# Probabilities times values of a forgetting attention: one plain fp32 pass in two halves of the array in place of a split in high and low parts

## The chip, the cores and the metric

One NeuronCore of a Trainium2 chip (trn2) runs the whole program. The metric is the device time of one execution in microseconds (us); lower is better. Engines are named as the profile names them: PE (TensorE, matmuls), PEld (its weight loads), DVE (VectorE), ACT (ScalarE), POOL (GpSimd), SP (the queue that issues most DMAs).

## What is computed

The reference is one layer of a hybrid block over 2048 tokens of width 1024, all in float32: RMSNorm, one wide input projection, and three branches (a forgetting attention, a complex state-space layer with a gated unit, a cross-attention into 256 memory tokens), which are gated, projected, merged and added to the input. The change lies in the forgetting attention, with 12 heads of width 64:

```python
def block(args):                                   # 128 queries of all heads
    qi, Fi, s0 = args
    s = jnp.einsum('bhqd,bhkd->bhqk', qi, kh)
    s = s + Fi[..., None] - F[:, :, None, :]       # F: running sum of log forget gates
    s = jnp.where(key_pos[None, :] <= qpos[:, None], s, NEG)
    p = jax.nn.softmax(s, axis=-1)
    return jnp.einsum('bhqk,bhkd->bhqd', p, vh)    # the product that is changed
```

## The kernel before

**Precision.** Nearly every product is done with operands split into two float32r parts, high and low (`hi` is a copy in that type, `lo` the rest). `mm3` (L147 to L149) issues hi*hi, hi*lo and lo*hi into one sum in PSUM. These three lines are most of the program's matmuls.

**Stages.** The input projection fills the first part; the state-space branch, its gated unit and the memory attention ride along in it. Then the forgetting attention runs, with the last projection chunks (`gen_gl`) and a first part of the merge (`gen_merge0`) as filler between its steps, and the rest of the merge and the output projection end the program. The forgetting attention holds 1628 to 2540 us of the span in the profile below.

**The attention.** `gen_fox` goes through heads and, in a head, through groups G = 7 to 0 of 256 queries, so 96 groups. For a group, `fox_scores` makes two blocks of 128 queries: matmuls into `psA` (L750, L751), the bias and the row maximum on DVE (L752), the exponential on ACT (L757), the division on POOL (L761). One group later `fox_pv` multiplies the probabilities with the values. It takes the keys in pairs `kp` of two tiles of 128 keys (even tile a = 0, odd tile a = 1), G + 1 pairs for group G, so 432 pairs in the program:

- PE transposes the probabilities of a pair into `psB` (L782; up to four transposes of 128x128).
- ACT copies them as high parts into `Pt` (L785; L790 for the last pair, which the causal mask cuts), and DVE subtracts to get the low parts (L786, L791).
- PE multiplies per key tile (L798): the weights are the tile's values `v`, 64 columns of high parts beside 64 of low parts; what streams is 512 columns of `Pt`, high parts of 256 queries, then low parts. All four products of parts land in the 128 partitions of `psC`; 864 matmuls, one for each key tile. For the last odd tile only the later 128 queries are streamed (256 columns).
- At the end of a group the four quarters are added: L801 (ACT), L802 (DVE), L804 (ACT), L805 (POOL); then comes the gate (L806, POOL) and a DMA.

In this stage `psA` and `psB` have three buffers, `psC` has one (`PS2`). The values are written to DRAM by `proj_v` (48 DMAs `s_vs<-ev_v`) and read back by `fox_keys` (24 DMAs `v<-s_vs`).

**What sets the order.** Each engine runs its own instructions in program order. The code's generators interleave attention and filler by constants (`PACE`, `LAG`, `DUE`), and the tile framework then orders each engine's instructions by a simulated timeline, so a change of one operation moves others too.

**A place that the prediction uses.** In `s5_pair` of the state-space branch a plain fp32 product already runs with 64 columns of weights, its results in the lower and the upper half of PSUM's partitions (L583 to L586):

```python
for g in range(2):
    for ri in range(2):
        nc.tensor.matmul(pv[64 * g:64 * g + 64, ri * 256:(ri + 1) * 256],
                         m1t[:, ri * 128 + 64 * g:ri * 128 + 64 * g + 64], u[:, g, :], start=True, stop=True)
```

All four are 128x64 weights by 128x256 data; the calls run 24 times, so these are 96 matmuls, and the trace has 192 instructions of them: a plain fp32 matmul is carried out as two. In the program's order the four of a call stand together four times; in the other 20 calls the two small matmuls of L572 (16 columns of weights) stand between, 14 times after the second of them, 6 times after the first. L625 and L626 are plain fp32 products over the full 128 columns.

Of the kernel before, what the change touches and what calls it, by code (L numbers as in the profile page):

```python
# [49 lines left out]
class Layer:  # L50
# [17 lines left out]
    def setup(self):  # L68
        nc, i = self.nc, self.i
        self.const, self.close_const = self.pool("const", side="right")  # L70
        self.wp, self.close_wp = self.pool("wp", side="right")
        self.ps, self.close_ps = self.pool("ps", space=PSUM)
        c = self.const
        self.eps = c.tile([128, 1], F32, name="eps")
        nc.vector.memset(self.eps, EPS)
        warm = c.tile([128, 1], F32, name="warm")
        nc.scalar.activation(warm, self.eps, AF.Sqrt)
        self.ident = c.tile([128, 128], F32, name="ident")
        nc.scalar.dma_start(out=self.ident, in_=i["ident"])
        self.g1 = c.tile([128, KD], F32, name="g1")  # L80
        nc.scalar.dma_start(out=self.g1, in_=i["g_norm"])
        self.identb = c.tile([128, 128], BF16, name="identb")
        nc.vector.tensor_copy(self.identb, self.ident)
        pw = self.psC()
        for n in range(WARM):
            nc.tensor.matmul(pw[:, :128], self.identb, self.identb, start=True, stop=True)
        s = {}
        for n, sh, dt in (
            ("qh", [DF, L], F32), ("ql", [DF, L], F32), ("kh", [DF, L], F32), ("kl", [DF, L], F32),
            ("vs", [H, 16, 128, 128], F32), ("gf", [DF, L], F32), ("gs", [DF, L], F32),  # L90
            ("gl", [3 * D, L], F32), ("gm", [DM, L], F32), ("qmh", [DM, L], F32), ("qml", [DM, L], F32),
            ("u", [6, 8, 128, 256], F32), ("kd", [48, 16, 128], F32), ("nf", [H, L], F32), ("yx", [DF, L], F32), ("yc", [6, 8, 128, 256], F32),
            ("ys", [DF, L], F32), ("ym", [DM, L], F32),
            ("mkh", [128, HM, ML], F32), ("mkl", [128, HM, ML], F32),
            ("mvh", [128, 2, DM], F32), ("mvl", [128, 2, DM], F32),
        ):
            s[n] = self.dram("s_" + n, sh, dt)
        self.s = s
# [35 lines left out]
    def load_w(self, src, shape, pool=None, bufs=2):  # L134
        """One [128, 1024] slab of weights, split into two float32r parts."""
        raw = self.wp.tile([128, 4 * NV], F32, tag="wraw", name="wraw", bufs=2)
        k, m = shape
        n = k * m
        self.nc.sync.dma_start(out=raw[:, :n], in_=src)
        hi, lo = ((pool or self.wp).tile([128, n if bufs == 1 else 1024], F32R, tag=t, name=t, bufs=bufs) for t in ("whi", "wlo"))  # L140
        self.split(hi[:, :n], lo[:, :n], raw[:, :n])
        return (hi[:, :n].rearrange("p (k m) -> p k m", k=k), lo[:, :n].rearrange("p (k m) -> p k m", k=k))

    def mm3(self, out, a, b, first, last):
        """a = (hi, lo) stationary, b = (hi, lo) moving."""
        nc = self.nc
        nc.tensor.matmul(out, a[0], b[0], start=first, stop=False)  # L147
        nc.tensor.matmul(out, a[0], b[1], start=False, stop=False)  # L148
        nc.tensor.matmul(out, a[1], b[0], start=False, stop=last)  # L149

    def rsqrt(self, p, out, ssq, n):
        """out = 1 / sqrt(ssq / D + eps): table square root, then a Newton step."""
# [11 lines left out]
    def norm_T(self, src, nt, g, hi, lo, p, xb, split=False):  # L164
        """RMSNorm of nt tiles of 128 tokens, then transposed and split: hi, lo [128, KD, nt*128]."""
# [90 lines left out]
    def proj_v(self, g, p):  # L256
        """Values of four heads; the forget gates ride with the first four."""
# [5 lines left out]
        for t in range(16):  # L263
# [7 lines left out]
            o = self.ev.tile([128, 4, 128], F32R, tag="ehi", name="ev_v", bufs=2)  # L271
            pv = ps[:, :256].rearrange("p (h d) -> p h d", h=4)
            nc.scalar.copy(o[:, :, 0:64], pv)
            nc.vector.tensor_sub(o[:, :, 64:128], pv, fl32(o[:, :, 0:64]))
            nc.sync.dma_start(out=s["vs"][g * 4:(g + 1) * 4, t].rearrange("h p d -> p h d"), in_=fl32(o))
# [12 lines left out]
    def forget(self, p):  # L288
        """-F, the running sum of -log sigmoid(z)."""
# [118 lines left out]
    def s5_exp(self, p, out, x):  # L408
        """exp(x): range reduction by ln 2, polynomial, exact power of two."""
# [15 lines left out]
    def s5_reduce(self, t, n):  # L425
        """t - 2 pi round(t / 2 pi), in place."""
        v = self.nc.vector
        v.tensor_scalar(out=n, in0=t, scalar1=0.15915494309189535, scalar2=12582912.0, op0=ALU.mult, op1=ALU.add)
        v.tensor_scalar(out=n, in0=n, scalar1=-12582912.0, scalar2=None, op0=ALU.add)
        for c in (6.28125, 2029.0 / 1048576.0, 3.0199159819e-7):  # L430
            v.scalar_tensor_tensor(out=t, in0=n, scalar=-c, in1=t, op0=ALU.mult, op1=ALU.add)

    def s5_sincos(self, p, sn, cs, t, n):
        """sin and cos of t in [-pi, pi] (t is overwritten) by the quarter angle and two doublings."""
# [17 lines left out]
    def cmul(self, outr, outi, ar, ai, br, bi, t):  # L452
        """(outr, outi) = (ar, ai) (br, bi); t is scratch; the outputs are none of the inputs."""
# [8 lines left out]
    def s5_prep(self, q, p):  # L462
        """Discretised parameters in the layout [(group parity, state), group pair]; q keeps, p is scratch."""
# [70 lines left out]
    def s5_pair(self, q, a):  # L534
        """Groups 2a and 2a+1. Chunks of 8 steps: what a chunk adds to the state (M1), the state at each chunk's
        end (a real scan of the states turned back by the phase they have run through), and the outputs from the
        state before the chunk (M2) and from the chunk's own inputs (M3)."""
# [168 lines left out]
    def fox_keys(self, h, c):  # L706
        """Half a head's keys (high over low parts), values (high beside low) and -F."""
# [3 lines left out]
        v = p.tile([128, 8, 128], F32R, tag="v", name="v", bufs=3)  # L711
# [4 lines left out]
        nc.sync.dma_start(out=fl32(v), in_=s["vs"][h, c * 8:(c + 1) * 8].rearrange("t p d -> p t d"))  # L716
# [13 lines left out]
    def fox_scores(self, p, hd, q, G, P):  # L730
        """Softmax rows of two blocks of 128 queries, the later one first: the mask goes into -F for good, as no
        later block of queries is left to read those keys unmasked."""
# [32 lines left out]
    def fox_pv(self, p, h, hd, G, P):  # L765
        """Columns of the moving operand and of the sums: high parts of the two query blocks, then low parts."""
# [6 lines left out]
        for kp in range(G + 1):  # L773
            ps = self.psB()
            t = p.tile([128, 2, 512], F32R, tag="Pt", name="Pt", bufs=3)
            hi, lo = t[:, :, 0:256], t[:, :, 256:512]
# [6 lines left out]
            psv = ps.rearrange("p (a n) -> p a n", a=2)  # L783
            if kp < G:
                nc.scalar.copy(hi, psv)  # L785
                nc.vector.tensor_sub(lo, psv, fl32(hi))  # L786
            else:
                for a in range(2):
                    c = slice(a * 128, 256)
                    nc.scalar.copy(hi[:, a, c], psv[:, a, c])  # L790
                    nc.vector.tensor_sub(lo[:, a, c], psv[:, a, c], fl32(hi[:, a, c]))  # L791
            for a in range(2):
                kt = 2 * kp + a
                v = hd[kt // 8][1][:, kt % 8, :]
                o, m = po, t[:, a, :]
                if kt == 2 * G + 1:
                    o, m = (z.rearrange("p (x b n) -> p x b n", x=2, b=2)[:, :, 1, :] for z in (o, m))
                self.pe = nc.tensor.matmul(o, v, m, start=(kt == 0), stop=(kt == 2 * G + 1))  # L798
            yield
        t = p.tile([128, 256], F32, tag="ot", name="ot", bufs=1)  # L800
        nc.scalar.copy(t, po[:, 256:512])  # L801
        nc.vector.tensor_add(t, po[:, 0:256], t)  # L802
        o = p.tile([64, 256], F32, tag="oo", name="oo", bufs=2)
        nc.scalar.copy(o, t[64:128])  # L804
        nc.gpsimd.tensor_add(o, o, t[0:64])  # L805
# [3 lines left out]
    def gen_fox(self):  # L809
        """Heads one after the other, groups of queries from the last to the first; a head's last KS groups, the  # L810
        short ones, alternate with the next head's first ones."""
# [75 lines left out]
    def split(self, hi, lo, x, sc=1.0):  # L887
        """sc * x as hi + lo, each exact in float32r."""
# [8 lines left out]
    def ytile(self):  # L897
        """Slots of 4 KB, twelve in the first pool and ten in the second, in the order in which they come free."""
# [21 lines left out]
    def gen_merge0(self):  # L920
        """The last chunk, under the last heads; its share of the attention as soon as the last head is past it."""
# [131 lines left out]
# The channels of the state-space branch are kept, 128 at a time, in the order (channel of a group, group).  # L1053
# [69 lines left out]
```

## Time and profile before

| what | us |
|---|---|
| median of 3 runs | 3076.02 (3070.25 to 3080.53) |
| the profiled execution: span from first to last instruction | 3072.7 |
| PE busy | 2995.7 (97% of the span) |
| DVE, ACT, POOL busy | 1884.8, 927.8, 1004.8 |
| L798, the matmuls that are replaced | 864 instructions |

For the profiled execution the page gives the span alone; the median of the timed runs is 3.3 us above it. A row of a group reads: line, engine, operation, output <- inputs, partitions x elements, count, busy us, mean ns of one; then the idle time of the engine ahead of it. A row of the timeline reads: start, duration, engine, line, operation, operands, weights' rows * columns, data's partitions x columns, count of merged neighbours. Matmuls are pipelined: the duration of one (some 0.39 us for 512 columns) overlaps the next, so what a matmul costs on PE is the distance from its start to the next one's start.

### The profile page before, as it was taken

Reading aid. Unit: us, or ns where it says so; the run is one execution under the profiler, and the core shown is the slowest. Engines: PE = TensorE matmul, PEld = TensorE weight load, DVE = VectorE, ACT = ScalarE, POOL = GpSimd, SP = SyncE. Lnnn points to the kernel's source line nnn. Section 1 sums busy time; section 2 is a strip of 40 time slices with the busy share of each in tenths; the row PEclk is TensorE's granted clock in tenths of the full one; section 3 lists DMA queues with packets and bytes.
Section 4 is the critical chain, followed back from the end, with each engine's and each line's share of the span. In section 5 each row is a group of like instructions: output and inputs, shape, how many; then the busy total and the mean of one; then the engine's idle time right before and its main releaser. Section 6 shows DMA issues by size and latency. Waiting matters only on the chain.

```text
span 3072.7 us, 43527 instructions
## 1 busy us (share of the span) xinstructions
PE 2995.7 (97%) x14656; PEld 2438.1 (79%) x14656; DVE 1884.8 (61%) x4982; ACT 927.8 (30%) x1881; POOL 1004.8 (33%) x1328
## 2 busy tenths in 40 slices
PE   9999999999999999999999999999999998999999
PEld 7889977777777778888878888888887786777787
DVE  5333489888886673322217777777777886555544
ACT  5102111111112231222216666666666550000011
POOL 0010000000001332121205665655555766555500
PEclk9999999999999999999999999999999998999999
DMA  5343323323344655344352443544434536665531
GB/s 167 107 136 96 105 84 116 115 84 111 114 132 150 175 164 173 108 127 136 115 165 82 124 121 103 134 121 121 118 111 130 145 108 195 185 182 172 159 108 69
DMA packets 283118, 396.81 MB, mean 129 GB/s; under 512 B 83060, under 2 KB 147828, under 8 KB 282884
## 3 DMA queue, kind: packets, MB, share of 16 engines
q1 hardware_dynamic: 275696, 381.39, 41.8%
q10 hardware_dynamic: 7200, 12.66, 1.2%
q8 instruction: 116, 1.90, 0.3%
q14 instruction: 106, 0.87, 0.1%
HBM read 265.51 MB, written 128.42 MB: 128 GB/s over the span
## 4 chain that ended last, share of the span: by engine, by line
PE 80%; DMA 6%; DVE 5%; issue 4%; POOL 3%; ACT 1%; SPq 0%; DVEq 0%; POOLq 0%; ACTq 0%
PE psF L147 10%; PE psF L148 10%; PE psF L149 10%; PE psA L147 8%; PE psA L148 8%; PE psA L149 8%; PE psC L798 5%; PE psB L782 5%; PE psA L750 3%; PE psA L751 3%; PE psC L147 1%; PE psC L148 1%; PE psC L149 1%; PE psC L585 1%; PE psB L149 1%
## 5 line engine op out<-in xcount | busy, mean ns | idle before, releaser
L147 PE MATMUL psF<-hh,whi 128*128 128x512 f32 (+1 forms) x1160 | 470.2, 405 | 5.3 <-DVE elo L228 2.5
L889 POOL TENSOR_SCALAR whi<-wraw 128x1024 fp32r<-128x1024 f32 (+2 forms) x216 | 204.8, 949 | 795.2 <-PE psA L148 362.0
L149 PE MATMUL psF<-hh,wlo 128*128 128x512 f32 (+1 forms) x1160 | 460.5, 397 | 0.5 <-DVE wlo L891 0.5
L148 PE MATMUL psF<-hl,whi 128*128 128x512 f32 (+1 forms) x1160 | 460.7, 397 | 0.0
L891 DVE TENSOR_TENSOR wlo<-wraw,whi 128x1024 fp32r<-128x1024 f32 (+2 forms) x216 | 260.5, 1207 | 213.4 <-POOL whi L889 189.2
L147 PE MATMUL psA<-hh,whi 128*128 128x512 f32 (+1 forms) x816 | 322.5, 397 | 1.4 <-ACT hh L187 0.8
L148 PE MATMUL psA<-hl,whi 128*128 128x512 f32 (+1 forms) x816 | 322.9, 396 | 0.0
L149 PE MATMUL psA<-hh,wlo 128*128 128x512 f32 (+1 forms) x816 | 321.7, 395 | 0.8 <-DVE wlo L891 0.8
L786 DVE TENSOR_TENSOR Pt<-psB,Pt 128x512 fp32r<-128x512 f32 x336 | 226.2, 685 | 76.3 <-ACT Pt L785 73.9
L798 PE MATMUL psC<-Pt,v 128*128 128x512 f32 x864 | 266.7, 398 | 4.1 <-DVE Pt L786 3.5
L147 PEld LDWEIGHTS psF<-hh,whi 128*128 128x128 f32 x1160 | 219.6, 189 | 52.7 <-DVE elo L228 3.3
L149 PEld LDWEIGHTS psF<-hh,wlo 128*128 128x128 f32 x1160 | 219.5, 189 | 52.0 <-DVE wlo L891 0.9
L148 PEld LDWEIGHTS psF<-hl,whi 128*128 128x128 f32 x1160 | 219.8, 189 | 45.8 <-issue 0.4
L752 DVE CUSTOM_DVE_ANT_0 P<-psA,nf 128x512 f32<-128x512 f32 (+1 forms) x336 | 201.2, 627 | 48.1 <-PE psA L751 28.2
L785 ACT CAST Pt<-psB 128x512 fp32r<-128x512 f32 x336 | 191.9, 586 | 107.4 <-PE psB L782 60.4
L761 POOL TENSOR_SCALAR P<-P,rd 128x768 f32<-128x768 f32 (+1 forms) x240 | 193.2, 821 | 59.6 <-DVE rd L758 36.6
L750 PE MATMUL psA<-kk,qh 128*128 128x512 f32 (+1 forms) x480 | 184.1, 389 | 4.5 <-DVE mx L752 2.6
L147 PEld LDWEIGHTS psA<-hh,whi 128*128 128x128 f32 x816 | 154.1, 189 | 36.9 <-issue 1.6
L149 PEld LDWEIGHTS psA<-hh,wlo 128*128 128x128 f32 x816 | 154.5, 189 | 36.1 <-DVE wlo L891 1.2
L148 PEld LDWEIGHTS psA<-hl,whi 128*128 128x128 f32 x816 | 154.3, 189 | 33.9 <-issue 0.4
L798 PEld LDWEIGHTS psC<-Pt,v 128*128 128x128 f32 x864 | 154.2, 190 | 31.2 <-DVE Pt L786 6.8
L782 PE MATMUL psB<-ident,P 128*128 128x128 f32 x1200 | 177.4, 274 | 0.3 <-POOL P L761 0.2
(343 smaller groups left out, 6228.3 us busy)
## 6 DMA issues: line engine op xcount, KB each, us to landing
wraw<-in_w_in SPq DMA_DIRECT2D x90, 512.0 KB, 4.3
s_gl<-ehi SPq DMA_DIRECT2D x96, 256.0 KB, 2.5
g<-s_gl SPq DMA_DIRECT2D x96, 256.0 KB, 4.6
wraw<-in_w_proj SPq DMA_DIRECT2D x64, 320.0 KB, 2.9
s_vs<-ev_v SPq DMA_DIRECT2D x48, 256.0 KB, 2.7
nf<-s_nf SPq DMA_DIRECT2D x24, 512.0 KB, 6.4
v<-s_vs SPq DMA_DIRECT2D x24, 512.0 KB, 6.4
qh<-s_qh SPq DMA_DIRECT2D x96, 128.0 KB, 3.7
```

Source lines behind the costliest of these rows:

```text
L147: nc.tensor.matmul(out, a[0], b[0], start=first, stop=False)
L148: nc.tensor.matmul(out, a[0], b[1], start=False, stop=False)
L149: nc.tensor.matmul(out, a[1], b[0], start=False, stop=last)
L750: nc.tensor.matmul(ps[:, :wm], q[0][:, qs], kk[:, c0:c0 + wm], start=True, stop=False)
L752: nc.vector.tensor_tensor_reduce(out=pr[:, c * 512:c * 512 + w], in0=ps[:, :w], in1=nf[:, c0:c0 + w], scale=1.0, scalar=-3.0e38, op0=ALU.a ...
L761: nc.gpsimd.tensor_scalar(out=c, in0=c, scalar1=rd, scalar2=0.5, op0=ALU.mult, op1=ALU.mult)
L782: nc.tensor.transpose(ps[:, o:o + 128], P[b][:, kt * 128:(kt + 1) * 128], self.ident)
L785: nc.scalar.copy(hi, psv)
L786: nc.vector.tensor_sub(lo, psv, fl32(hi))
L798: self.pe = nc.tensor.matmul(o, v, m, start=(kt == 0), stop=(kt == 2 * G + 1))
L889: self.nc.gpsimd.tensor_scalar(out=hi, in0=x, scalar1=sc, scalar2=1.0, op0=ALU.mult, op1=ALU.mult)
L891: self.nc.vector.tensor_sub(lo, x, fl32(hi))
```

## The change

The values and the probabilities are no longer split. `Pt` is one fp32 copy of the transposed probabilities, made by ACT for even `kp` and by DVE for odd `kp`; the weights are the 64 fp32 columns of the values; the matmul of the even tile writes the lower 64 partitions of `psC` and that of the odd tile the upper 64, both over 256 columns of queries. At a group's end ACT copies the upper half and DVE adds the lower one. The value tiles and their transfers are half as wide. (Docstrings are gone too; they are left out here.)

```diff
-            ("vs", [H, 16, 128, 128], F32), ("gf", [DF, L], F32), ("gs", [DF, L], F32),
+            ("vs", [H, 16, 128, 64], F32), ("gf", [DF, L], F32), ("gs", [DF, L], F32),
...
-            o = self.ev.tile([128, 4, 128], F32R, tag="ehi", name="ev_v", bufs=2)
-            pv = ps[:, :256].rearrange("p (h d) -> p h d", h=4)
-            nc.scalar.copy(o[:, :, 0:64], pv)
-            nc.vector.tensor_sub(o[:, :, 64:128], pv, fl32(o[:, :, 0:64]))
-            nc.sync.dma_start(out=s["vs"][g * 4:(g + 1) * 4, t].rearrange("h p d -> p h d"), in_=fl32(o))
+            o = self.ev.tile([128, 4, DH], F32, tag="ehi", name="ev_v", bufs=2)
+            nc.scalar.copy(o, ps[:, :256].rearrange("p (h d) -> p h d", h=4))
+            nc.sync.dma_start(out=s["vs"][g * 4:(g + 1) * 4, t].rearrange("h p d -> p h d"), in_=o)
...
-        v = p.tile([128, 8, 128], F32R, tag="v", name="v", bufs=3)
+        v = p.tile([128, 8, DH], F32, tag="v", name="v", bufs=3)
...
-            t = p.tile([128, 2, 512], F32R, tag="Pt", name="Pt", bufs=3)
-            hi, lo = t[:, :, 0:256], t[:, :, 256:512]
+            t = p.tile([128, 2, 256], F32, tag="Pt", name="Pt", bufs=4)
...
+            copy = nc.vector.tensor_copy if kp % 2 else nc.scalar.copy
             if kp < G:
-                nc.scalar.copy(hi, psv)
-                nc.vector.tensor_sub(lo, psv, fl32(hi))
+                copy(t, psv)
             else:
                 for a in range(2):
-                    c = slice(a * 128, 256)
-                    nc.scalar.copy(hi[:, a, c], psv[:, a, c])
-                    nc.vector.tensor_sub(lo[:, a, c], psv[:, a, c], fl32(hi[:, a, c]))
+                    copy(t[:, a, a * 128:256], psv[:, a, a * 128:256])
             for a in range(2):
                 kt = 2 * kp + a
-                v = hd[kt // 8][1][:, kt % 8, :]
-                o, m = po, t[:, a, :]
-                if kt == 2 * G + 1:
-                    o, m = (z.rearrange("p (x b n) -> p x b n", x=2, b=2)[:, :, 1, :] for z in (o, m))
-                self.pe = nc.tensor.matmul(o, v, m, start=(kt == 0), stop=(kt == 2 * G + 1))
+                c = slice(128 if kp == G and a else 0, 256)
+                self.pe = nc.tensor.matmul(po[64 * a:64 * a + 64, c], hd[kt // 8][1][:, kt % 8, :], t[:, a, c],
+                                           start=(kp == 0), stop=(kp == G))
             yield
-        t = p.tile([128, 256], F32, tag="ot", name="ot", bufs=1)
-        nc.scalar.copy(t, po[:, 256:512])
-        nc.vector.tensor_add(t, po[:, 0:256], t)
         o = p.tile([64, 256], F32, tag="oo", name="oo", bufs=2)
-        nc.scalar.copy(o, t[64:128])
-        nc.gpsimd.tensor_add(o, o, t[0:64])
+        if G:
+            nc.scalar.copy(o, po[64:128, 0:256])
+        else:
+            nc.gpsimd.memset(o[:, 0:128], 0.0)
+            nc.scalar.copy(o[:, 128:256], po[64:128, 128:256])
+        nc.vector.tensor_add(o, po[0:64, 0:256], o)
         nc.gpsimd.tensor_mul(o, o, gf)
```

How it stands in the program's order, first on PE, in the second group of the first head (L798 is the product, L782 the transposes, L750/L751 the scores of the next group, L147 to L149 the filler). Before:

```order
L798 MATMUL psC<-Pt,v 128x512 x2
L782 MATMUL psB<-ident,P 128x128 x4
L750 MATMUL psA<-kk,qh 128x256
L751 MATMUL psA<-kk,ql 128x256
L798 MATMUL psC<-Pt,v 128x512
L750 MATMUL psA<-kk,qh 128x512
L751 MATMUL psA<-kk,ql 128x512
L782 MATMUL psB<-ident,P 128x128 x4
L798 MATMUL psC<-Pt,v 128x2x128
L782 MATMUL psB<-ident,P 128x128 x4
```

The same group after the change (line numbers have moved: L790 is the product, L779 the transposes, L748/L749 the scores):

```order
L790 MATMUL psC<-Pt,v 64x256 x6
L779 MATMUL psB<-ident,P 128x128 x4
L748 MATMUL psA<-kk,qh 128x256
L749 MATMUL psA<-kk,ql 128x256
L147 MATMUL psF<-hh_154,whi 128x512
L148 MATMUL psF<-hl_155,whi 128x512
L790 MATMUL psC<-Pt,v 64x256 x2
L779 MATMUL psB<-ident,P 128x128 x3
L149 MATMUL psF<-hh_154,wlo 128x512
```

The product now writes 64 partitions by 256 columns and stands in pairs: even and odd tile follow each other, where before one of them often stood alone. Counted over the whole program, the 864 products stand in 389 uninterrupted stretches before and in 273 after: 174 of one pair, 53 of two, 25 of three, 19 of four, and 2 single ones. Of the 273, 86 follow a transpose and 187 a matmul of the scores or the filler; 181 are followed by a transpose and 92 by a matmul of the scores or the filler. In 176 of the stretches the last product streams 256 columns.

On DVE, at the end of the third group, before (L786 and L791 make low parts, L802 adds at a group's end, L752 is the bias and maximum of the scores):

```order
L786 TENSOR_TENSOR Pt<-psB,Pt 128x2x256
L756 TENSOR_REDUCE nm<-mx 128x1
L786 TENSOR_TENSOR Pt<-psB,Pt 128x2x256
L802 TENSOR_TENSOR ot<-psC,ot 128x256
L786 TENSOR_TENSOR Pt<-psB,Pt 128x2x256
L758 RECIPROCAL rd<-den 128x1
L752 ISA P,mx<-psA,nf 128x512
```

The same end of a group after (L783 is the copy of an odd pair, L799 the add, L750 the bias and maximum):

```order
L783 COPY Pt<-psB 128x512
L756 RECIPROCAL rd<-den 128x1
L799 TENSOR_TENSOR oo<-psC,oo 64x256
L750 ISA Ps,mx<-psA,nf 128x384
L750 ISA mx 128x1
L754 TENSOR_REDUCE nm<-mx 128x1
L783 COPY Pt<-psB 128x512
```

DVE no longer takes part in every pair, only in odd ones, and reads `psB` there without waiting for ACT.

More of the change, by code (lines that the diff above doesn't have):

```diff
@@ L715, in fox_keys @@
         nc.sync.dma_start(out=nf, in_=s["nf"][h:h + 1, ks].partition_broadcast(128))
-        nc.sync.dma_start(out=fl32(v), in_=s["vs"][h, c * 8:(c + 1) * 8].rearrange("t p d -> p t d"))
+        nc.sync.dma_start(out=v, in_=s["vs"][h, c * 8:(c + 1) * 8].rearrange("t p d -> p t d"))
         return kk, v, nf
```

## The prediction

> **What bounds the kernel now.** I read the page first, then PE's rows stretch by stretch, then what PE waits for in the attention, and last the starts of single matmuls. From the page: the span, PE's busy share, PE's granted clock, the chain that ended last.
>
> ```profile
> span 3072.7 us, 43527 instructions
> PE 2995.7 (97%) x14656; PEld 2438.1 (79%) x14656; DVE 1884.8 (61%) x4982; ACT 927.8 (30%) x1881; POOL 1004.8 (33%) x1328
> PEclk9999999999999999999999999999999998999999
> PE 80%; DMA 6%; DVE 5%; issue 4%; POOL 3%; ACT 1%; SPq 0%; DVEq 0%; POOLq 0%; ACTq 0%
> ```
>
> PE runs nearly all the time at full clock, and four fifths of the chain are its own work. The busy time in three stretches (columns: length, then busy time and count of PE, PEld, DVE, ACT, POOL) shows the same for the attention, the middle row:
>
> ```profile
> 0.00:1628.00 1628.00, 1605.59 (x7848) 1306.70 (x7848) 919.27 (x2570) 337.30 (x660) 220.29 (x319) 0.99 0.42 127
> 1628.00:2540.00 912.00, 892.71 (x4781) 740.66 (x4780) 673.05 (x1999) 562.51 (x1140) 557.98 (x795) 0.99 0.43 119
> 2540.00:3072.70 532.70, 497.43 (x2028) 390.70 (x2028) 292.53 (x415) 27.97 (x82) 226.53 (x215) 0.96 0.49 152
> ```
>
> PE is idle there for 912.0 - 892.7 = 19.3 us; DVE is free for a quarter of the stretch, ACT and POOL for more. So a microsecond added to PE's work there is a microsecond of the span, and one taken from DVE or ACT is worth at most what PE waits for them. The list of PE's waits in that stretch:
>
> ```profile
> PE psF L147 <- POOL ymg L889: 4.9, 5, 2.2
> PE psC L798 <- DVE Pt L786: 3.5, 2, 2.7
> PE psF L148 <- DVE ymg L891: 3.0, 2, 2.0
> PE psA L750 <- DVE mx L752: 2.6, 2, 2.3
> ```
>
> The low parts of the probabilities (L786) cost PE 3.5 us in all, the row maximum (L752) 2.6 us.
>
> **The product's own work.** The groups that go, and the starts of matmuls that give their price (the second column is a pipelined duration; I use distances between starts):
>
> ```profile
> L798 PE MATMUL psC<-Pt,v 128*128 128x512 f32 x768 | 240.9, 409 | 4.1 <-DVE Pt L786 3.5 <-DVE Pt L791 0.2
> L798 PE MATMUL psC<-Pt,v 128*128 128x256 f32 x96 | 30.0, 313 | 0.0
> ...
> 447.42 0.39 PE L147 MATMUL psF<-hh,whi 128*128 128x512 f32 x1
> 447.66 0.39 PE L148 MATMUL psF<-hl,whi 128*128 128x512 f32 x1
> 447.89 0.39 PE L149 MATMUL psF<-hh,wlo 128*128 128x512 f32 x1
> 448.12 0.40 PE L147 MATMUL psF<-hh,whi 128*128 128x512 f32 x1
> 448.45 1.08 PE L585 MATMUL psC<-u,m1t 128*64 128x256 f32 x4
> 449.46 0.61 PE L572 MATMUL psB<-z,bb 128*16 128x128 f32 x4
> ```
>
> A float32r matmul over 512 columns starts 0.233 us after the one ahead ((448.12 - 447.42) / 3). So the product costs 768 x 0.233 + 96 x 0.117 (half the columns) = 190.2 us now. What replaces it is plain fp32 over 256 columns, which PE carries out as two instructions. Full-width ones of that kind are here:
>
> ```profile
> 417.67 0.59 PE L625 MATMUL psC<-u,m 128*128 128x256 f32 x2
> 418.10 0.59 PE L626 MATMUL psC<-hs,z 128*128 128x256 f32 x2
> 418.53 0.59 PE L625 MATMUL psC<-u,m 128*128 128x256 f32 x2
> ```
>
> 0.43 us for each matmul, 0.215 for each instruction. Alone that would be dear: 0.43 us for a key tile against 0.233. What decides is whether the two halves run side by side. The state-space branch has the new form exactly (128*64 weights, 128x256 data, both halves): once with its four matmuls together in the program (eight instructions), elsewhere cut in two (four instructions of one stretch):
>
> ```profile
> 405.27 1.09 PE L585 MATMUL psC<-u,m1t 128*64 128x256 f32 x8
> 406.29 0.33 PE L551 MATMUL psB<-ident,m1i 128*128 128x128 f32 x1
> 406.37 0.48 PE L147 MATMUL psA<-hh,whi 128*128 128x512 f32 x1
> 406.69 0.40 PE L148 MATMUL psA<-hl,whi 128*128 128x512 f32 x1
> ...
> 767.29 1.08 PE L585 MATMUL psC<-u,m1t 128*64 128x256 f32 x4
> 768.30 0.50 PE L147 MATMUL psF<-hh,whi 128*128 128x512 f32 x1
> 768.64 0.39 PE L148 MATMUL psF<-hl,whi 128*128 128x512 f32 x1
> ```
>
> Eight instructions, four for each half, hold PE from 405.27 to 406.29, 1.02 us; four in one half, from 767.29 to 768.30, 1.01 us. So the halves do run side by side, and a pair of key tiles costs one matmul's 0.43 us: 432 x 0.432 = 186.6 us. (In the cut pairs the odd tile's 128 columns hide beside the even tile's 256.) The product's own work changes by -3.6 us, next to nothing.
>
> **The switch.** The rows show a second price. From the last full-width matmul to the first of 64 columns passes 448.45 - 448.12 = 0.33 us, 0.09 more than 0.233. The stretch of four takes 1.01 us, from its first start to the next line's, 0.146 more than 4 x 0.216. And the first full-width matmul behind takes 768.64 - 768.30 = 0.34 us, 0.106 more; behind a stretch that is followed by a transpose, transpose and matmul together take 406.69 - 406.29 = 0.40 us, where 0.109 + 0.233 = 0.34 is usual, 0.058 more. Nothing overlaps as the array changes its width. Now transposes and full-width products follow each other without that, as here, where seven transposes and four products take 1.70 us, which is 7 x 0.109 + 4 x 0.233:
>
> ```profile
> 1905.08 0.93 PE L782 MATMUL psB<-ident,Ps 128*128 128x128 f32 x7
> 1905.76 1.18 PE L798 MATMUL psC<-Pt,v 128*128 128x512 f32 x4
> 1906.78 0.39 PE L147 MATMUL psF<-hh,whi 128*128 128x512 f32 x1
> ```
>
> The changed program has 273 stretches of products. In and out cost 0.093 + 0.146 = 0.239 us each, 65.2 us; the slow first one behind 181 x 0.058 = 10.5 us (transposes) and 92 x 0.106 = 9.8 us (others). Together 85.5 us, in the stretch where PE has no room. Unknown is the entry behind a transpose (86 stretches), which no row shows; I take the same price, since that of L572's narrow 128-column matmul into L585 is alike. Without any entry price for these it would be 86 x 0.144 = 12.4 us less, and without the slow first ones 20.3 us less.
>
> **The other parts.** DVE and ACT lose work:
>
> ```profile
> L786 DVE TENSOR_TENSOR Pt<-psB,Pt 128x512 fp32r<-128x512 f32 x335 | 225.6, 685 | 76.3 <-ACT Pt L785 73.9
> L785 ACT CAST Pt<-psB 128x512 fp32r<-128x512 f32 x333 | 190.3, 586 | 107.4 <-PE psB L782 60.4 <-PE psC L798 41.7 <-DVE mx L752 2.2
> L805 POOL TENSOR_TENSOR oo<-oo,ot 64x256 f32<-64x256 f32 x95 | 73.4, 772 | 41.4 <-ACT oo L804 41.1
> ```
>
> All subtractions go and about half the copies move from ACT to DVE; a copy on DVE has no row, but should not pass the subtraction's 0.685 us. Between transposes and product stands one step of at most 0.69 us in place of 0.586 + 0.685 = 1.27 us. That takes the 3.5 us of L798's wait and, with DVE freer, I count L752's 2.6 us as gone: -6.1 us. The bounds are 0 and all PE idle time, -19.3 us. POOL's add at a group's end goes (73 us, off the path). The release of the one `psC` buffer stays two steps, ACT then DVE. The value transfers halve, beside a DMA share of 0.42, with as many issues on SP's queue as before; in the projections the subtraction for the values goes, which PE's row in full (1605.6 of 1628) hides. Moved filler I count as nothing: its amount is the same, and PE pays for it wherever it stands.
>
> **Sum.** -3.6 + 85.5 - 6.1 = +75.8 us on the span of 3072.7, so 3148.5; the median of the runs lies 3.3 above the span, so 3152 us, 2.5% slower. (0.3%, 9 us, is about what a measurement of this kernel can tell from no change.)
>
> **A rule of the Trainium skill.** The page "TensorE: Matmul & The Clock Gate", Part 3, says that matmuls keep strict first-in-first-out order in start and end, tiles or not. The eight instructions in 1.02 us speak against it: in that order (four of one half, then four of the other) only one would overlap, and they would take seven steps, 1.5 us. The same part of that page of the Trainium skill ("Measured speedup vs the span model") gives the span of packed tiles as one matmul's duration and some 4 ns for each further tile, with no price for changing the width; the rows above have one.
>
> **Rivals.** *Instructions stay in order.* If in the new stretches the odd tile's second instruction has to wait for its first, as in strict order, a stretch of n pairs takes 2n + 1 steps: 0.216 us more for each of the 176 stretches whose last product has 256 columns, +38 us: 3190 us. For it: none of the measured cases alternates halves, nor adds into sums. Against: the row of eight. *Halves one after the other.* If something the state-space product lacks (the accumulation, a wait of the odd tile's own) keeps them apart, the work is about 352 us in place of 187: 3317 us. *The switch is hidden.* If the array changes its width at no price, the product's work falls by 3.6 us and the waits by 6.1: 3066 us, faster by 0.3%. It decides once a switch costs less than 9.7 / 273 = 0.036 us. For it: PE could fetch the next weights while the array empties. Against: the 0.09 us before L585 and the 0.106 us after it. *New waits.* Fewer, longer stretches need several pairs' copies at once; if PE's idle time in the attention doubles in place of falling, it is +19.3 + 6.1: 3177 us.
>
> **How the numbers follow.** The forecast 0.69 (its own range 3120 to 3175), new waits 0.08, strict order 0.10, one after the other 0.05, the switch hidden 0.05, and 0.03 for a switch so cheap that no difference shows. The range goes down by the entry (12.4), the slow first ones (20.3) and the rest of the waits (13.2) to 3106, up to strict order with new waits in part, 3208. Slower holds the first four cases, 0.92; same 0.03; faster 0.05.
>
> **What would show it.** In the profile after: the product's rows 128*64, 1728 instructions, the two halves' starts within some 20 ns of each other and 0.216 us between steps; 0.33 us ahead of a stretch and 0.34 us for the matmul behind it; PE's idle time in the attention no more than 20 us, and the attention some 75 us longer with the stages around it unchanged. DVE's busy time falls by over 100 us and the span does not care. Wrong it would be if stretches entered from transposes cost nothing, or if a pair took 0.65 or 0.86 us.

## The result and the profile after

The changed kernel takes 3116.76 us (median; 3113.14 to 3118.42), the kernel before 3075.83 us over the runs on both occasions: ratio 1.0137, interval 1.0118 to 1.0155. It is slower by 41 us where the forecast said 76 us, inside the range. Two parts of the page, the busy times and the clock:

```profile
span 3116.6 us, 44285 instructions
PE 3054.4 (98%) x15520; PEld 2364.1 (76%) x15520; DVE 1734.6 (56%) x4646; ACT 797.2 (26%) x1545; POOL 925.9 (30%) x1244
PEclk9999999999999999999999999999999999999999
```

DVE lost 150 us of work, ACT 131, POOL 79, and the span grew by 43.9 us. PE at full clock is still what counts. The busy times in the attention, now 1621 to 2583 us (columns as in the prediction), show PE idle for 5 us:

```profile
1621.00:2583.00 962.00, 957.00 (x5628) 672.07 (x5628) 537.58 (x1710) 431.94 (x806) 481.25 (x711) 1.00 0.38 107
```

And the list of PE's waits in that stretch has only two rows left (us in total, times, longest):

```profile
PE psF L147 <- DVE g L939: 4.7, 2, 3.1
PE psB L779 <- POOL P L759: 0.3, 1, 0.3
```

The new product's two groups:

```profile
L790 PE MATMUL psC<-Pt,v 128*64 128x256 f32 x1536 | 245.9, 395 | 0.0
L790 PE MATMUL psC<-Pt,v 128*64 128x128 f32 x192 | 39.4, 287 | 0.0
```

1536 + 192 = 1728 instructions, as expected. One long stretch of it in PE's timeline, sixteen instructions for four pairs:

```profile
1903.94 0.60 PE L779 MATMUL psB<-ident,Ps 128*128 128x128 f32 x4
1904.47 1.95 PE L790 MATMUL psC<-Pt,v 128*64 128x256 f32 x16
1906.35 0.65 PE L779 MATMUL psB<-ident,Ps 128*128 128x128 f32 x4
```

From 1904.47 to 1906.35 pass 1.88 us: eight steps, in each of them one instruction of either half, 8 x 0.216 = 1.73 us, and 0.15 us for the switch (the array's change to 64 columns and back). Had the halves not run together it would be twice 1.73 us.

**An account by distances.** To see where the time went I give every matmul its usual distance to the next (0.233 us for 512 float32r columns, 0.109 for a transpose, 0.216 for a plain fp32 instruction of 256 columns; for the stretches of 64 columns what they really took with entry and exit), add these up, and call what is left over PE's waits. The sums are good to some 5 us.

| us | product | waits ahead of the attention | in it | behind it |
|---|---|---|---|---|
| before | 190.4 | 47.3 | 34.7 | 53.7 |
| after | 276.9 | 40.2 | 3.6 | 49.6 |
| difference | +86.5 | -7.1 | -31.1 | -4.1 |

The sum is +44.2 us, the spans differ by 43.9. So the new product costs PE what was forecast, and nearly half of it comes back from waits. The 3.6 us are too low: PE's idle time by durations, 5 us, is already more. Counted gap by gap (every step that is over 0.05 us longer than usual), the waits in the attention are 35.2 us before and 8.8 after; by that, some 26 us went in place of 31, and the product costs some 5 us less than 276.9.

### The profile page after: what moved, and what is told of

Same layout as the page of the kernel before. It is cut to its first block, busy times and chain, and to the rows that moved or that the text cites. A ratio compares the mean times of both kernels' runs of the same rounds, so it can differ in the third digit from the quotient of the medians.

```text
span 3116.6 us, 44285 instructions
## 1 busy us (share of the span) xinstructions
PE 3054.4 (98%) x15520; PEld 2364.1 (76%) x15520; DVE 1734.6 (56%) x4646; ACT 797.2 (26%) x1545; POOL 925.9 (30%) x1244
## 4 chain that ended last, share of the span: by engine, by line
PE 86%; DMA 5%; DVE 3%; POOL 2%; issue 2%; ACT 0%; SPq 0%; DVEq 0%; POOLq 0%; ACTq 0%
PE psF L147 10%; PE psF L148 10%; PE psF L149 10%; PE psA L147 8%; PE psA L149 8%; PE psA L148 8%; PE psC L790 7%; PE psB L779 6%; PE psA L748 3%; PE psA L749 3%; PE psC L148 1%; PE psC L147 1%; PE psC L149 1%; PE psC L583 1%; DMA s_ys<-gs 1%
## 5 line engine op out<-in xcount | busy, mean ns | idle before, releaser
L147 PE MATMUL psF<-hh,whi 128*128 128x512 f32 (+1 forms) x1160 | 468.7, 404 | 3.2 <-DVE elo L228 2.5
L149 PE MATMUL psF<-hh,wlo 128*128 128x512 f32 (+1 forms) x1160 | 460.2, 397 | 0.5 <-DVE wlo L885 0.5
L147 PE MATMUL psA<-hh,whi 128*128 128x512 f32 (+1 forms) x816 | 322.3, 397 | 2.9 <-POOL whi L883 1.9
L149 PE MATMUL psA<-hh,wlo 128*128 128x512 f32 (+1 forms) x816 | 320.7, 394 | 0.6 <-DVE wlo L885 0.6
L147 PEld LDWEIGHTS psF<-hh,whi 128*128 128x128 f32 x1160 | 218.6, 188 | 62.8 <-issue 14.9
L750 DVE CUSTOM_DVE_ANT_0 P<-psA,nf 128x512 f32<-128x512 f32 (+1 forms) x336 | 201.9, 629 | 112.3 <-PE psA L749 103.8
L149 PEld LDWEIGHTS psF<-hh,wlo 128*128 128x128 f32 x1160 | 218.5, 188 | 50.5 <-issue 1.1
L790 PE MATMUL psC<-Pt,v 128*64 128x256 f32 x1728 | 246.3, 383 | 0.0
L755 ACT ACTIVATE P<-P,nm 128x2048 f32<-128x2048 f32 (+3 forms) x96 | 156.7, 1632 | 143.1 <-DVE nm L754 142.8
L748 PE MATMUL psA<-kk,qh 128*128 128x512 f32 (+1 forms) x480 | 185.9, 391 | 0.9 <-ACT ehi L238 0.8
L147 PEld LDWEIGHTS psA<-hh,whi 128*128 128x128 f32 x816 | 153.6, 189 | 38.4 <-POOL whi L883 2.9
L149 PEld LDWEIGHTS psA<-hh,wlo 128*128 128x128 f32 x816 | 153.9, 189 | 35.6 <-issue 1.0
L779 PEld LDWEIGHTS psB<-ident,P 128*128 128x128 f32 x1200 | 135.2, 141 | 59.8 <-issue 39.3
L779 PE MATMUL psB<-ident,P 128*128 128x128 f32 x1200 | 175.1, 278 | 0.4 <-POOL P L759 0.4
L749 PE MATMUL psA<-kk,ql 128*128 128x512 f32 (+1 forms) x480 | 175.1, 370 | 0.0
```

Source lines behind the costliest of these rows:

```text
L748: nc.tensor.matmul(ps[:, :wm], q[0][:, qs], kk[:, c0:c0 + wm], start=True, stop=False)
L749: nc.tensor.matmul(ps[:, :wm], q[1][:, qs], kk[:, c0:c0 + wm], start=False, stop=True)
L750: nc.vector.tensor_tensor_reduce(out=pr[:, c * 512:c * 512 + w], in0=ps[:, :w], in1=nf[:, c0:c0 + w], scale=1.0, scalar=-3.0e38, op0=ALU.a ...
L755: nc.scalar.activation(pr[:, :nk], pr[:, :nk], AF.Exp, bias=nm, accum_out=den)
L779: nc.tensor.transpose(ps[:, o:o + 128], P[b][:, kt * 128:(kt + 1) * 128], self.ident)
L790: self.pe = nc.tensor.matmul(po[64 * a:64 * a + 64, c], hd[kt // 8][1][:, kt % 8, :], t[:, a, c], start=(kp == 0), stop=(kp == G))
```

## The experiments

Theory L says that the waits in the attention went because ACT and DVE have less to do and the chain from transpose to product is shorter. Theory S says that PE, slowed by the switches, simply waits less for an unchanged feed. The medians below stand beside runs of the kernel before on the same chip; the time of an edit counts against those.

**Lighter ACT and DVE, old product.**

```diff
-            hi, lo = t[:, :, 0:256], t[:, :, 256:512]
+            hi = p.tile([128, 2, 256], F32R, tag="Pt", name="Pt", bufs=4)
...
+            copy = nc.vector.tensor_copy if kp % 2 else nc.scalar.copy
             if kp < G:
-                nc.scalar.copy(hi, psv)
-                nc.vector.tensor_sub(lo, psv, fl32(hi))
+                copy(hi, psv)
...
+                m = m.unsqueeze(1).to_broadcast([128, 2, m.shape[1]])
```

> The kernel before with its float32r product of 512 columns per key tile, but ACT and DVE make only the one rounded copy of the probabilities, in turn as in the changed kernel; the matmul streams that copy twice (the low parts of the probabilities are left out). PE's work is that of before, 190 us for the product, no change of width. Theory L (the waits of PE in the attention, 36 us by distances between starts, came from the load and the chain of ACT and DVE): they go, 3076 - 30 = 3046 us (3036 to 3055). Theory S (PE, slowed by the switches, merely waits less for an unchanged feed): the waits stay, 3065 to 3076 us.

Measured: 3046.45 us, 3070.96 before, ratio 0.9915 (0.9898 to 0.9931). By the account the product is unchanged (190.4 us) and the waits in the attention are 8.9 us in place of 34.7. The lighter load alone, with PE's work unchanged, takes 26 us of them. That is L. The edit holds three things at once, as the change does: less work on ACT and DVE, one step less between transpose and product, and four buffers `Pt` in place of three. The program's order moved too (289 stretches of products in place of 389). No run separates these.

**More work on PE, old load.**

```diff
+                if a == 0:
+                    nc.tensor.matmul(po[:, 0:448], v, t[:, 0, 0:448], start=False, stop=False)
```

> The kernel before with one more float32r matmul of 448 columns for each pair of key tiles, into the same sums (which counts part of the products twice): 432 x 0.204 = 88 us more work on PE, ACT and DVE as before. Theory L: the waits stay, 3076 + 88 = 3164 us (3155 to 3170). Theory S: the added work covers them, 3076 + 88 - 30 = 3134 us (3125 to 3145).

Measured: 3140.54 us, ratio 1.0224 (1.0207 to 1.0241): +70 us for 88 us of work, between the two and nearer to S. The waits in the attention fall to 12.3 us with ACT and DVE as heavily loaded as before. So a slower PE alone takes 22 us of them. Either is enough to remove most of them; both together (the changed kernel) can't take more than there is.

**The changed kernel with the old load.**

```diff
+            h = p.tile([128, 2, 256], F32R, tag="Ph", name="Ph", bufs=3)
+            def copy(out, src):
+                ph = h if kp < G else h[:, a, a * 128:256]
+                nc.scalar.copy(ph, src)
+                nc.vector.tensor_tensor(out=out, in0=src, in1=fl32(ph), op=ALU.max)
```

> The changed kernel with the load of before put back: ACT makes a rounded copy of every pair of tiles, DVE then writes the operand from PSUM and that copy (the larger of the two, which changes the probabilities' last bits), so both engines and the chain from transpose to product are as before. The program's order has 344 stretches of products in place of 273, which at 0.31 us each adds 22 us. Theory L: the waits come back, 3117 + 22 + 30 = 3169 us (3155 to 3180). Theory S: 3117 + 22 = 3139 us (3130 to 3150).

Measured: 3161.77 us, ratio 1.0291 (1.0276 to 1.0306). The total fits L, but for another reason. In the account the product takes 315.0 us, 38 more than in the changed kernel: of the 344 stretches 125 are single products, which have no other half to run beside, so more was lost than the 22 us for the switches. The waits in the attention are 5.5 us, as in the changed kernel. They did not come back (gap by gap 11.2 against 8.8 us): with this product and this order PE is slow enough to cover them under the old load too. By the account the old load costs its time here by way of the order, in which the products stand in more and shorter stretches. Without the account this run would have been read the wrong way.

**Both tiles in one half.**

```diff
-                self.pe = nc.tensor.matmul(po[64 * a:64 * a + 64, c], hd[kt // 8][1][:, kt % 8, :], t[:, a, c],
-                                           start=(kp == 0), stop=(kp == G))
+                self.pe = nc.tensor.matmul(po[0:64, c], hd[kt // 8][1][:, kt % 8, :], t[:, a, c],
+                                           start=(kt == 0), stop=(kt == 2 * G + 1))
```

> The changed kernel with both key tiles of a pair in the lower half of the partitions, in one running sum (the upper half is not used; the odd sums are replaced by the lower ones at the end, so the result is doubled). Same number of matmuls, 281 stretches. If the halves run side by side in the changed kernel, the product's work grows from 187 to 352 us here: 3117 + 165 + 3 = 3285 us (3265 to 3295). If they did not, the time stays at 3117 to 3125 us.

Measured: 3278.54 us, ratio 1.0671 (1.0645 to 1.0698). The timeline shows a stretch of eight instructions that takes as long as the sixteen above, 1905.32 - 1903.45 = 1.87 us:

```profile
1903.45 1.94 PE L790 MATMUL psC<-Pt,v 128*64 128x256 f32 x8
1905.32 0.55 PE L779 MATMUL psB<-ident,P 128*128 128x128 f32 x3
```

The two halves are worth 162 us in the changed kernel by the medians, 167 when each run counts against the kernel before on its own chip; without them it would be far behind.

**Full width, plain fp32.**

```diff
+                vv = hd[kt // 8][1].rearrange("p t d -> p (t d)")[:, kt % 8 // 2 * 128:kt % 8 // 2 * 128 + 128]
+                self.pe = nc.tensor.matmul(po[:, c], vv, t[:, a, c], start=(kt == 0), stop=(kt == 2 * G + 1))
```

> The changed kernel with weights of 128 columns: each product takes the values of both key tiles of a pair side by side and writes all 128 partitions, in one running sum (half of what it adds is the wrong tile's, so the sums mix products). Plain fp32 and the number of matmuls stay; the width of the array never changes, and nothing runs side by side. If the price of a stretch belongs to the change of width: product 768 x 0.432 + 96 x 0.216 = 352 us without any switch, in place of 277: 3117 + 75 = 3192 us (3180 to 3200). If it belongs to going from float32r to fp32 and back: 281 x 0.31 = 87 us more, 3279 us.

Measured: 3201.92 us (ratio 1.041, 1.0389 to 1.0432), 2 us outside what was expected for the width and 77 us under the other. The timeline shows a stretch of twelve instructions, the products of six key tiles, between float32r matmuls:

```profile
1897.75 0.39 PE L749 MATMUL psA<-kk,ql 128*128 128x512 f32 x1
1897.98 2.75 PE L791 MATMUL psC<-Pt,v 128*128 128x256 f32 x12
1900.38 0.58 PE L147 MATMUL psF<-hh,whi 128*128 128x512 f32 x1
1900.80 0.40 PE L148 MATMUL psF<-hl,whi 128*128 128x512 f32 x1
```

It starts 0.23 us after the float32r matmul ahead, as another of that kind would. To the second matmul behind it pass 1900.80 - 1897.98 = 2.82 us, which is 12 x 0.216 + 0.233, with nothing on top (the matmul behind starts early and takes as much longer). The 64-column stretches pay ahead, inside and behind.

So the price of a stretch belongs to the change of width, not to the type.

**Longer stretches.** Two kernels issue the products of four pairs, or of a whole group, together. The core of the second:

```diff
-        for kp in range(G + 1):
+        for kp in range(G, -1, -1):
...
+            held.append((kp, t))
+            if kp % 8 == 0:
+                for kq, tq in reversed(held):
+                    for a in range(2):
...
```

> The changed kernel with the products of up to four pairs of a group issued together: the pairs of a batch are transposed and copied from the last to the first, then multiplied from the first to the last, so that all operands lie ready when the first product may run; eight buffers for them in place of four. The program has 129 stretches of products in place of 273. The switch at 0.312 us each saves 144 x 0.312 = 45 us: 3072 us. Theory L (waits went with the load of ACT and DVE, which is unchanged here): 3072 us (3064 to 3080). Theory S (the slower PE covered them): part of 30 us comes back, 3080 to 3100 us. If the switch were not the price, 3117 us.

> The same with the products of a whole group together, up to eight pairs, nine buffers: 97 stretches in place of 273. The switch saves 176 x 0.312 = 55 us. Theory L: 3062 us (3053 to 3072), which would be under the kernel before. Theory S: 3075 to 3095 us. Waits of its own for the nine buffers would show as PE waiting for copies.

Measured: 3084.68 us and 3082.98 us, both with ratio 1.0038 to before (intervals 1.0024 to 1.0052 and 1.0023 to 1.0052), some 30 us faster than the changed kernel (each against the kernel before on its chip). By the account the product falls from 276.9 us to 228.0 and 218.3: 49 and 59 us for 144 and 176 stretches fewer, 0.34 us each. The switch was sized right. The totals come out at 3083 to 3085 us all the same, within what Theory S expected, because other waits grew: some 8 us behind the attention with four pairs and with eight, and with eight also 21.2 us in it in place of 3.6. (The profiled execution with eight, 3089.44 us, is the slowest of its five, so part of that may be its own.) The list of PE's waits in the attention of the kernel with groups of eight shows the filler's operands again:

```profile
PE psF L147 <- POOL ymg L888: 4.7, 2, 2.4
PE psF L147 <- DVE g L944: 4.5, 2, 4.2
PE psA L748 <- DVE mx L750: 1.4, 3, 0.8
PE psA L748 <- DMA qh<-s_qh: 1.3, 3, 0.7
```

The group kernels have the light load of the changed one; PE alone got faster. That waits return in the attention with eight pairs speaks for S; that they do not with four speaks against it as the whole account. Both orders differ in more than the pace, so these runs don't decide it.

**Half the product's work.**

```diff
+                c = slice(128 if kt == 2 * G + 1 else 0, 256)
+                o, m = po[:, c], hi[:, a, c]
...
+        nc.scalar.copy(o, po[64:128, 0:256])
+        nc.vector.tensor_add(o, po[0:64, 0:256], o)
```

> The kernel before with the rounded copy of the probabilities streamed once, 256 columns (the low parts of the probabilities are left out), ACT and DVE making the copies in turn, and the group's end as in the changed kernel. Full width, float32r. PE's product work is 95 us in place of 190. If PE's waits went only with the lighter load of ACT and DVE, they stay away: 3046 - 95 = 2951 us (2943 to 2958). If they also depend on PE's pace, they come back as PE gets faster: up to 30 us of them, 2960 to 2985 us.

Measured: 2982.57 us, 3077.84 before, ratio 0.9696 (0.9679 to 0.9714). The product takes 95.2 us, and the waits in the attention are 32.5 us, as many as before the change, though ACT and DVE carry the light load. What PE waits for in the attention has changed, by the list of its waits there: queries from DRAM stand first, where it was the filler's operands and the low parts.

```profile
PE psA L750 <- DMA qh<-s_qh: 5.1, 3, 2.6
PE psA L751 <- DMA ql<-s_ql: 3.7, 3, 2.6
PE psB L781 <- POOL P L761: 2.0, 2, 1.6
PE psB L781 <- DVE Pt L785: 1.8, 1, 1.8
```

This one is 3% faster than the kernel before, and faster than the changed one too, at the price of the probabilities' low parts: it keeps the full width and the fast type and streams half the columns. It isn't the same computation to the same precision, so it is no replacement for either without a decision on that.

The waits in the attention follow neither load nor pace alone. In us, with the length of the attention (from the start of the first product to the end of the last):

| kernel | ACT and DVE load | product | attention | waits in it |
|---|---|---|---|---|
| before | old | 190.4 | 909 | 34.7 |
| lighter ACT and DVE | light | 190.4 | 878 | 8.9 |
| half the work | light | 95.2 | 806 | 32.5 |
| more work on PE | old | 278.6 | 974 | 12.3 |
| changed, old load | old | 315.0 | 1001 | 5.5 |
| changed | light | 276.9 | 961 | 3.6 |
| groups of eight | light | 218.3 | 913 | 21.2 |
| groups of four | light | 228.0 | 911 | 5.7 |

Gap by gap, the same waits fall into kinds by the matmul that starts late (us):

| kernel | product | scores | transposes | filler | sum |
|---|---|---|---|---|---|
| before | 8.4 | 8.4 | 3.0 | 15.4 | 35.2 |
| lighter ACT and DVE | 0.2 | 4.1 | 0.9 | 4.3 | 9.5 |
| half the work | 0.7 | 15.2 | 5.9 | 5.9 | 27.8 |
| more work on PE | 2.3 | 3.1 | 0.4 | 8.1 | 13.8 |
| changed, old load | 1.0 | 3.6 | 0.8 | 5.8 | 11.2 |
| changed | 0.3 | 0.2 | 0.5 | 7.8 | 8.8 |
| groups of eight | 1.2 | 7.5 | 2.2 | 11.5 | 22.4 |

Only a quarter of the waits before stand ahead of the product. With the light load these are gone whatever PE's pace, even where PE has half the product's work; with a slower PE alone 6 of the 8 us are gone. The other kinds move with PE's pace and with the order: in the half-work run they are mostly waits for queries from DRAM and for POOL's probabilities, as the list above shows.

## Why the prediction was right, and where it missed

**The bound** was right: PE's work in the attention decides, at full clock; 130 to 150 us taken from ACT and DVE bought only waits.

**The product's own work** was right: side by side in all stretches of whole pairs. The first instructions of both tiles start 7 ns apart or less in the changed kernel, 14 ns or less in the state-space branch, and both tiles in one half cost the 162 to 167 us more that the one-half run shows.

**The switch** was right in kind and nearly in size: forecast 85.5 us on 273 stretches. Measured, the product with its switches takes 276.9 us, 90 more than the 186.6 of its work. Entry was 0.093 us behind transposes and full-width matmuls alike (median of 86 and 187), which answers the one open price; a stretch of one pair took 0.583 us to the next line's start, 0.151 over its work; the exit cost 0.104 us in full-width matmuls and 0.06 with transposes. That the product fell by 0.34 us for each of the 144 or 176 stretches removed confirms it.

**The waits** were the step that failed. The prediction took 6.1 us off and named 19.3 us, PE's idle time in the attention, as the bound; the account finds 34.7 us there, of which 31.1 went (26 gap by gap), and 11 more elsewhere. The reading was at fault, and with it both numbers. A matmul's recorded duration of 0.39 us covers the distance of 0.233 us to the next and 0.16 us beyond it, so every gap loses up to that much to "busy": the list of waits and the busy share see only the rest. (Of the 35.2 us in 112 gaps, 20.2 us lie beyond the first 0.16 us of their gap, close to the 19.3 us idle.) Ahead of the product stood 8.4 us of waits where the list has 3.5, and the waits of the scores and the filler, of which 2.6 us were counted, lost some 16. The prediction said itself that distances between starts are what a matmul costs, and then measured idleness by durations. With 34.7 us gone in place of 6.1 the sum would have been 3123 us.

**That the range held** was luck in part. Its lower end, 3106 us, counts on an entry behind transposes and a slow first matmul that cost nothing, and both cost what the forecast said. With the waits alone the range would have ended at 3152 - 13.2 = 3139 us, above the 3117 measured, and the forecast's own range, 3120 to 3175 us, misses it. (The 12.4 us for the entry are a slip besides: 86 x 0.093 is 8.0 us, and no row gives 0.144.)

**Why the waits went** had two causes, and the prediction named only one. The run with the light load alone takes 26 us of them, that with the slow PE alone 22 us, so most would have gone with either part of the change by itself; and in the half-work run, light load and fast PE, they stand at 32.5 us. "DVE freer" was half of the answer; PE itself being later was the other. Each of these edits also moved the program's order, and no run holds the order fixed.

**Moved filler and the value projection** were counted as nothing. The waits ahead of the attention are 7 us lower; in the kernels with unsplit values they are 39 to 43 us, in those with split ones 47 to 52. They are spread over several places and no run separates the lighter projection from the order that came with it.

**The rivals.** Strict order, +38 us, is out by the starts: in all 53 single pairs with a cut odd tile, the odd tile's second instruction (128 columns) starts 0.10 us before the even tile's second one, which the program issues ahead of it; and the 121 single pairs without a cut take 0.58 us, where three steps with the switch would take some 0.8. The rule of the Trainium skill's page "TensorE: Matmul & The Clock Gate", Part 3, that matmuls keep strict order in start and end, does not hold here for the starts of two column halves; the ends are modelled in the profile and show nothing either way. One half after the other costs 3279 us, not 3117. The hidden switch is out by the account and by the full-width run. New waits did not appear in the changed kernel; they did in the groups of eight.

## What to carry to other kernels

Before a change on the bounding engine is priced, add up the distances between starts in the stage, not busy time: what is left over is what a slower or better fed engine may give back. Here that was about a third of what the new product added. A pair of plain fp32 matmuls of 64 columns, one in each half, took as long here as one of 128 columns (0.43 us), but each time the array goes to the narrow width and back costs some 0.3 us, so count the stretches in the program's final order and make them few and of whole pairs. And where a total agrees with a theory, check the account: the loaded run agreed for another reason.

## What the runs showed of the hardware

- The two halves do not wait for each other between instructions: a half with shorter instructions starts its next one ahead of an earlier-issued one of the other half (by 0.10 us, 53 of 53 times).
- Going to 64 columns and back costs 0.093 us ahead, 0.15 us inside and 0.06 to 0.10 us behind, nearly the same each time (0.575 to 0.584 us inside for all 174 stretches of one pair), whatever stands ahead; plain fp32 at full width between float32r matmuls has no such price (2.82 us for twelve instructions and the matmul behind them, as their usual steps add up to).
- Accumulating into both halves of the partitions of one PSUM tile at once cost nothing that shows: the steps are 0.216 us, as in the state-space product, which does not accumulate.
